# A hybrid retention, attention and expert layer on one core: instruction order from deadlines, with gathers held and small steps moved between engines

## The chip, the cores and the metric

The kernel runs on one core of one Trainium2 chip. The metric is device time in microseconds (us), the median over runs. The core has five engines, each with a queue of its own that it works through in order: TensorE (PE; its weight loads are PEld) for matmuls, VectorE (DVE), ScalarE (ACT), GpSimd (POOL) and SyncE (SP), which here only issues DMAs. GpSimd also issues the indirect DMAs that fetch rows by index.

## The reference

One layer over 1024 latent tokens and 256 context tokens of width 1024, in float32. A modulated RMS norm feeds one projection, whose columns go to four heads of bidirectional retention and four heads of differential attention; both outputs are joined, projected and added with a gate. Then each token goes through a product-key expert layer with 8 retrieval heads, 16 experts each out of 128 x 128, and a gated residual.

```python
rq, rk, rv, rg, dq, dk, dv = split(modulate(x, norm1_g, ...) @ w_in)
ret = rms_norm(bidirectional_retention(...)) * silu(rg)
dif = (softmax(q1 k1) - lam * softmax(q2 k2)) v          # per head, then rms_norm
x = x + mod[2] * (concat(ret, dif) @ w_out)
h2 = modulate(x, norm2_g, ...)
def peer_ffn(hb):                                         # 128 tokens at a time
    q = (hb @ w_query).reshape(t, 8, 2, 128)
    s = einsum('thpc,hpnc->thpn', q, sub_keys)
    v1, i1 = top_k(s[:, :, 0], 16); v2, i2 = top_k(s[:, :, 1], 16)
    cand = v1[..., :, None] + v2[..., None, :]            # 256 sums, ids i1 * 128 + i2
    best, pos = top_k(cand, 16)
    experts, gate = cand_idx[pos], softmax(best)
    act = gelu(einsum('thkd,td->thk', expert_u[experts], hb))
    return einsum('thk,thkd->td', gate * act, expert_v[experts])
x = x + mod[5] * peer_ffn(h2)
```

## The kernel before

Tokens are worked on in blocks of 128: 8 latent blocks, 2 of context. The code does not call the engines itself: a recorder, `Plan`, takes every instruction with an estimated cost, its dependencies and a priority. `schedule()` then plays the engines through a model (costs, DMA time, buffers that come free), lets each idle engine take its ready instruction of the lowest priority value, and so writes down the order in which each engine's queue is filled. That one pass is the order that runs. The priority of an instruction is the matmul time recorded before it, so the order in which the parts are recorded, woven into one another by the spans QSPAN, ASPAN, GSPAN, HSPAN and so on, sets the order of the work. All instructions pass through one helper, which is why every row of the profile has line L497; rows are told apart by the names of their tiles.

The parts, in the order of time:

- Projections (`project_half`, `late_queries`) in three float32r products of high and low parts each; `qk` normalizes and rotates queries and keys; `f_rg` makes the SiLU of the retention gate by Exp on ScalarE and an add, a reciprocal and a product on VectorE (tile u), and stores it. `retention` follows.
- Per group of blocks (GROUPS = [0], [4,5], [6,7], [3], [1,2]): `mix` (attention, output projection, second norm) and `route` (query projection, then `top16` per head with VectorE's top-8 instructions, then `select`). `select` forms 50 candidate sums per head, takes the best 16 and finds their ids: VectorE compares a row of 0 to 49 with each found position (16 x 50 elements), GpSimd multiplies by the ids, VectorE sums; 8 times a block, in tile sel.
- Blocks 3 to 7 (DENSE) go through all 128 x 128 experts by matmul. For that `gates` builds, from the ids, a matrix of gate values: for four tokens at a time a compare of the low id (o2) and of the high id times the gate weight (o1), four matmuls, four ScalarE copies into staging tiles; after 32 tokens four stores to Wd in DRAM. o2 is made on ScalarE (Abs, Relu) for every other four tokens (O2A), else by one wide VectorE compare; o1 by four VectorE compare-and-scale instructions. Tiles o, t, and pt for the ids.
- Blocks 0, 1 and 2 gather their experts' rows: `halves` issues 768 indirect DMAs of 128 rows (512 KB) on GpSimd into tile gat (4 buffers; tile h lends some). For an expert's u row VectorE multiplies with the tokens and sums (gat<-gat,h2t), for its v row it adds a scaled row to acc (acc<-gat,act,acc). These have priorities of their own, by a pace (POFF, PACES).
- `dense_phase`: 128 steps in groups of 4. `dense_act` loads one 128-expert part of u, splits it into high (ScalarE) and low parts (VectorE, tile h, 1024 wide), multiplies, applies Gelu, multiplies by the gate rows, and splits the result into high (ScalarE) and low (CL = 'P': GpSimd; tiles rv, 384 wide, and t, 256 wide). `dense_val` does the same with v (tile h, 512 wide; VL = 'PDD': every third low part on GpSimd, the others on VectorE) and adds the products to b and t.

In the planner's cost model VectorE instructions with two inputs in SBUF and GpSimd's arithmetic exclude each other.

## Time and profile before

| what | before |
|---|---|
| median of 3 runs | 3646.94 us (3646.93 to 3651.82) |
| profiled execution, its own time | 3638.93 us |
| its span | 3637.1 us |
| TensorE busy | 3254.3 us (89%) |
| VectorE busy | 2945.7 us (81%) |
| GpSimd busy | 1750.9 us (48%) |
| ScalarE busy | 1258.8 us (35%) |
| mean granted TensorE clock | 0.935 of full |
| DMA | 809.72 MB, 223 GB/s |

An engine's busy share is an average over stages that have different limits, so it has to be read by stage. In a row of an instruction form the columns are the names of output and inputs, the shapes, the count, the busy time and the mean duration of one in ns, and then the idle time just before such instructions with what ended it. Idle time counts only on the engine that sets the pace.

### The profile page before, as it was taken

How to read it: one execution, taken by the hardware profiler on the slowest of the kernel's cores; microseconds unless marked ns; L12 is line 12 of the kernel's file. 1: busy time of each engine (PE TensorE's matmuls, PEld its weight loads, DVE VectorE, ACT ScalarE, POOL GpSimd, SP SyncE). 2: the span in 40 equal slices, each digit the busy share in tenths (PEclk: the TensorE clock that was granted, in tenths of full speed). 3: DMA queues.
4: the chain of work that ended last, by engine and by line, in shares of the span. 5: the costliest groups of instructions: out<-in, count | busy, mean ns of one | idle time of the engine just before them, and what ended most of it. 6: DMA issues, size and time to landing. Idle time of an engine off the chain costs nothing. (4 is left out here: it accounts for less than half of the span.)

```text
span 3637.1 us, 52106 instructions
## 1 busy us (share of the span) xinstructions
PE 3254.3 (89%) x18240; PEld 2793.0 (77%) x18240; DVE 2945.7 (81%) x5999; ACT 1258.8 (35%) x3210; POOL 1750.9 (48%) x1457
## 2 busy tenths in 40 slices
PE   7989987888778658777889999999999999999998
PEld 4987566566667646566878898888988889898897
DVE  4456547879999899989798988889898979888954
ACT  4342333324226546566432222222222222222221
POOL 0101122555462242332067775767667657686731
PEclk9999988889988869788999999999999999999999
DMA  5223544777555735547547888888888888888943
GB/s 179 81 83 98 167 165 149 239 246 263 174 182 201 255 124 195 198 159 265 165 135 257 295 286 284 271 306 293 295 303 275 306 270 291 303 290 300 301 145 110
DMA packets 314536, 809.72 MB, mean 223 GB/s; under 512 B 29313, under 2 KB 125593, under 8 KB 314274
## 3 DMA queue, kind: packets, MB, share of 16 engines
q1 hardware_dynamic: 203682, 403.70, 33.3%
q0 software_dynamic: 110592, 402.70, 32.2%
q8 instruction: 144, 2.36, 0.3%
q14 instruction: 118, 0.97, 0.1%
HBM read 745.46 MB, written 60.83 MB: 222 GB/s over the span
## 5 line engine op out<-in xcount | busy, mean ns | idle before, releaser
L497 PE MATMUL mm<-k,h 128*128 128x384 f32 (+1 forms) x4096 | 888.7, 308 | 3.7 <-DVE h L497 3.7
L497 PEld LDWEIGHTS mm<-k,h 128*128 128x128 f32 x4096 | 688.2, 188 | 5.9 <-DVE h L497 4.4
L497 ACT CAST h<-wst 128x512 fp32r<-128x512 f32 (+1 forms) x384 | 292.1, 763 | 1085.0 <-PE mm L497 963.2
L497 POOL DMA_INDIRECT gat<-peer_v,egb x363 | 471.5, 1299 | 347.7 <-DVE acc L497 187.1
L497 PE MATMUL mm<-v,h 128*128 128x384 f32 (+1 forms) x2048 | 633.0, 309 | 0.0
L497 POOL DMA_INDIRECT gat<-peer_u,egb x345 | 448.2, 1299 | 369.6 <-DVE gat L497 232.5
L497 PE MATMUL mm<-h,rv 128*128 128x512 f32 x2304 | 584.2, 397 | 13.7 <-POOL rv L497 9.2
L497 DVE SCALAR_TENSOR_TENSOR acc<-gat,act,acc 128x1024 f32<-128x1024 f32 x360 | 522.6, 1452 | 48.0 <-DMA gat<-peer_v,egb 42.9
L497 PEld LDWEIGHTS mm<-h,rv 128*128 128x128 f32 x2304 | 431.0, 189 | 121.5 <-POOL rv L497 14.9
L497 DVE SCALAR_TENSOR_TENSOR gat<-gat,h2t 128x1024 f32<-128x1024 f32 x345 | 481.0, 1397 | 51.9 <-DMA gat<-peer_u,egb 51.6
L497 PE MATMUL mm<-h,t 128*128 128x512 f32 (+1 forms) x1600 | 418.0, 394 | 14.0 <-DVE b L497 13.3
L497 DVE TENSOR_TENSOR h<-wst,h 128x512 fp32r<-128x512 f32 (+1 forms) x298 | 336.2, 1134 | 88.9 <-ACT h L497 61.6
L497 PEld LDWEIGHTS mm<-v,h 128*128 128x128 f32 x2048 | 385.0, 188 | 1.3
L497 PEld LDWEIGHTS mm<-h,t 128*128 128x128 f32 x1600 | 299.2, 189 | 88.3 <-DVE b L497 16.5
L497 POOL TENSOR_TENSOR m<-m,mhalf 128x4 f32<-128x4 f32 (+1 forms) x78 | 76.4, 980 | 439.9 <-DVE m L497 435.6
L497 POOL TENSOR_TENSOR rv<-aT,rv 128x384 fp32r<-128x384 f32 x128 | 154.5, 1207 | 242.5 <-ACT rv L497 234.9
L497 PE MATMUL mm<-b,wst 128*128 128x256 f32 (+1 forms) x1280 | 250.9, 354 | 9.1 <-ACT rv L497 9.1
L497 PEld LDWEIGHTS mm<-b,wst 128*128 128x128 f32 x1280 | 214.0, 201 | 40.9 <-ACT rv L497 9.6
L497 POOL TENSOR_TENSOR sel<-sel 128x800 f32<-128x800 f32 (+6 forms) x120 | 136.8, 1156 | 214.7 <-DVE sel L497 200.5
L497 ACT COPY rv<-mm 128x128 f32<-128x128 f32 (+2 forms) x664 | 178.3, 412 | 113.3 <-PE mm L497 97.4
L497 PE MATMUL mm<-t,h 128*128 128x256 f32 x992 | 187.5, 288 | 7.9 <-ACT aT L497 3.3
L497 PE MATMUL mm<-k,t 64*128 64x512 f32 (+1 forms) x384 | 174.2, 620 | 22.8 <-ACT h L497 13.2
(235 smaller groups left out, 5454.6 us busy)
## 6 DMA issues: line engine op xcount, KB each, us to landing
wst<-peer_u_cols SPq DMA_DIRECT2D x128, 512.0 KB
wst<-peer_v_halves SPq DMA_DIRECT2D x128, 512.0 KB
wst<-w_query_chunks SPq DMA_DIRECT2D x80, 512.0 KB
Wd<-rv SPq DMA_DIRECT2D x80, 512.0 KB
h<-Wd SPq DMA_DIRECT2D x64, 512.0 KB
wst<-w_mod_chunks SPq DMA_DIRECT2D x48, 512.0 KB
wst<-w_out_chunks SPq DMA_DIRECT2D x40, 512.0 KB
wst<-w_in_chunks SPq DMA_DIRECT2D x32, 512.0 KB
```

Of the source, the lines that this page charges most:

```text
L497: getattr(handles[n.eng], meth)(*[res(v) for v in a], **k)
```

## The change

Eight edits. (1) The priorities come from a plan: `plan()` runs `schedule()` up to four times (PASSES); after each, `ahead()` goes backwards through that pass and gives every instruction the mean of its start and its latest start, over dependencies and over buffers handed on; the pass with the shortest planned span is kept. The weaving spans are set anew. (2) While the planner's clock is between 1000 and 1600 us (HOLD), GpSimd may take no gather. (3) In `gates` both compares are one wide VectorE instruction each, and the gate weight is multiplied in by four ScalarE copies with a scale. (4) The staging tiles of `gates` alternate between rv and gat. (5) `f_rg` uses ScalarE's SiLU. (6) In `select` the ids are found by a keyed minimum: each candidate's id gets 32768 times its place added, 32768 times the found place is subtracted, and the minimum of the absolute value over 50 is the id; GpSimd's product falls away. (7) All low parts of the dense phase are on VectorE (VL, CL = 'D'). (8) `qk` and `head_norm` put their squares into SBUF rather than PSUM. The gathers have an order of buffers of their own (key rows); EXTRA is empty. No matmul is added or removed.

```diff
+STEP = 32768
+PASSES = 4
+HOLD = [1000, 1600]
+EXTRA = [[], [], []]
...
-QSPAN = [[-0.2, 0.475], [0.1, 1], [-0.2, 1.309], [-0.6, 1.05], [0, 0.85]]
+QSPAN = [[-0.2, 0.475], [0.1, 1], [-0.05, 1.309], [-0.35, 1.05], [0.15, 0.9]]
...
-VL, CL, EC, EM, XE = 'PDD', 'P', 'PD', 'P', 'PPPPPPPP'
+VL, CL, EC, XE = 'D', 'D', 'PD', 'PPPPPPPP'
...
-O2A = [0, 2, 4, 6]
...
@@ in schedule()
-                pick = None
+                pick, held = None, []
                 while avail[e]:
                     item = heapq.heappop(avail[e])
                     m = nodes[item[1]]
+                    if e == "POOL" and m.xfer and HOLD[0] <= t < HOLD[1]:
+                        held.append(item)
+                        continue
...
                 if pick is None:
+                    if held:
+                        heapq.heappush(events, HOLD[1])
...
+                n.done = done
...
+    def ahead(self, out):
+        left, freed, used, succ = {}, {}, {}, {}
+        for bs in self.order.values():
+            for b in bs:
+                left[id(b)] = len(b.nodes)
+        taken = set()
+        for n in out:
+            pred = set(n.deps)
+            for b in n.bases:
+                if b.dram or id(b) in taken:
+                    continue
+                taken.add(id(b))
+                used[b.tag] = used.get(b.tag, 0) + 1
+                if used[b.tag] > self.bufs.get(b.tag, 1):
+                    pred |= freed[b.tag].pop(0)
+            for b in n.bases:
+                if not b.dram:
+                    left[id(b)] -= 1
+                    if left[id(b)] == 0:
+                        freed.setdefault(b.tag, []).append(b.nodes)
+            for q in pred:
+                succ.setdefault(q, []).append(n)
+        latest = {}
+        for n in sorted(out, key=lambda n: (n.start, n.seq), reverse=True):
+            took = n.done - n.start
+            latest[n.seq] = min([self.span - took] + [latest[x.seq] - took - SEM for x in succ.get(n.seq, ())
+                                                      if x.seq in latest])
+        for n in out:
+            n.prio = (n.start + latest[n.seq]) / 2
+    def plan(self):
+        best = None
+        for i in range(PASSES):
+            if i:
+                self.ahead(out)
+                for bs in self.order.values():
+                    for b in bs:
+                        if b.lenders:
+                            b.tag = b.key
+            try:
+                out = self.schedule()
+            except RuntimeError:
+                break
+            tags = {id(b): b.tag for bs in self.order.values() for b in bs}
+            if best is None or self.span < best[0]:
+                best = (self.span, out, tags)
+        self.span, out, tags = best
+        for bs in self.order.values():
+            for b in bs:
+                b.tag = tags[id(b)]
+        return out
...
-        sch = self.schedule()
+        sch = self.plan()
...
+        steps = sb([128, NCAND], "steps")
+        nc.vector.tensor_scalar(steps, iota[:, :NCAND], float(STEP), None, op0=OP.mult)
...
         def f_rg(kb, pm, c):
-            t = sb([128, 256], "u4")
-            nc.scalar.activation(t, pm, AF.Exp, scale=-1.0)
-            nc.vector.tensor_scalar(t, t, 1.0, None, op0=OP.add)
-            nc.vector.reciprocal(t, t)
-            nc.vector.tensor_tensor(out=t, in0=t, in1=pm, op=OP.mult)
+            t = sb([128, 256], "fin")
+            nc.scalar.activation(t, pm, AF.Silu)
             nc.sync.dma_start(rgd[kb - NCB][:, c * 256:(c + 1) * 256], t)
...
         def qk(kb, pm, which, h0):
             m4 = sb([128, 2, 4], "m4")
-            sq = ps([128, 256])
-            nc.scalar.activation(sq, pm, AF.Square, scale=SC)
+            xn = sb([128, 256], "u1")
+            nc.scalar.activation(xn, pm, AF.Square, scale=SC)
...
         def head_norm(dst, src, gain):
-            sq = ps([128, 512])
-            nc.scalar.activation(sq, src, AF.Square)
+            nc.scalar.activation(dst, src, AF.Square)
...
-            nc.vector.tensor_copy(posf, pos)
+            nc.vector.tensor_scalar(posf, pos, float(STEP), None, op0=OP.mult)
+            nc.vector.tensor_tensor(out=cid, in0=cid, in1=steps[:, None, :].to_broadcast([128, PH, NCAND]), op=OP.add)
             for h in range(PH):
                 oh = sb([128, TK, NCAND], "sel")
-                nc.vector.tensor_tensor(out=oh, in0=iota50[:, None, :].to_broadcast([128, TK, NCAND]),
-                                        in1=posf[:, h, :, None].to_broadcast([128, TK, NCAND]), op=OP.is_equal)
-                eng(EM, h).tensor_tensor(out=oh, in0=oh, in1=cid[:, h:h + 1, :].to_broadcast([128, TK, NCAND]), op=OP.mult)
-                nc.vector.tensor_reduce(out=ef[:, h, :], in_=oh, axis=AX.X, op=OP.add)
+                nc.vector.tensor_tensor(out=oh, in0=cid[:, h:h + 1, :].to_broadcast([128, TK, NCAND]),
+                                        in1=posf[:, h, :, None].to_broadcast([128, TK, NCAND]), op=OP.subtract)
+                nc.vector.tensor_reduce(out=ef[:, h, :], in_=oh, axis=AX.X, op=OP.min, apply_absolute_value=True)
...
-        def gather(rows, table):
+        def gather(b, rows, table):
             t = sb([128, D], "gat")
-            t.base.lenders = LENDERS
+            t.base.key, t.base.lenders = "rows", LENDERS + EXTRA[b]
             nc.gpsimd.indirect_dma_start(out=t, out_offset=None, in_=table, in_offset=(rows,))
             return t
...
-                stage = [sb([128, 32, TG], "rv") for _ in range(4)]
+                stage = [sb([128, 32, TG], "gat" if g % 2 else "rv") for _ in range(4)]
                 for q in range(TG // 4):
                     t0 = g * TG + q * 4
                     o2 = sb([128, 4, 128], "t3" if q % 2 else "t6")
                     pm = ps([128, 4, 128])
-                    if q in O2A:
-                        for j in range(4):
-                            nc.scalar.activation(o2[:, j, :], iota, AF.Abs, scale=-1.0,
-                                                 bias=pt[:, 1, t0 + j:t0 + j + 1])
-                        nc.scalar.activation(o2, o2, AF.Relu, scale=-1.0, bias=1.0)
-                    else:
-                        nc.vector.tensor_tensor(out=o2, in0=iota[:, None, :].to_broadcast([128, 4, 128]),
-                                                in1=pt[:, 1, t0:t0 + 4, None].to_broadcast([128, 4, 128]),
+                    o1 = sb([128, 4, 128], "t4" if q % 2 else "o")
+                    for o, x in ((o1, 0), (o2, 1)):
+                        nc.vector.tensor_tensor(out=o, in0=iota[:, None, :].to_broadcast([128, 4, 128]),
+                                                in1=pt[:, x, t0:t0 + 4, None].to_broadcast([128, 4, 128]),
                                                 op=OP.is_equal)
-                    o1 = sb([128, 4, 128], "t4" if q % 2 else "o")
                     for j in range(4):
-                        t = t0 + j
-                        nc.vector.tensor_scalar(o1[:, j, :], iota, pt[:, 0, t:t + 1], pt[:, 2, t:t + 1],
-                                                op0=OP.is_equal, op1=OP.mult)
+                        nc.scalar.activation(o1[:, j, :], o1[:, j, :], AF.Copy, scale=pt[:, 2, t0 + j:t0 + j + 1])
                     with nc.unit():
                         for j in range(4):
                             nc.tensor.matmul(pm[:, j, :], o2[:, j, :], o1[:, j, :], start=True, stop=True)
```

## Rows read from the trace of the kernel before

**Rows 1.** Stretches: busy PE, PEld, DVE, ACT, POOL (instructions); clock, DMA share, GB/s
```profile
0.00:600.00 600.00, 534.53 (x3629) 437.78 (x3629) 310.34 (x837) 210.55 (x526) 73.82 (x101) 0.94 0.42 136
600.00:1800.00 1200.00, 922.24 (x4665) 743.29 (x4666) 1075.68 (x3090) 570.80 (x1770) 469.48 (x398) 0.84 0.59 204
1800.00:3637.00 1837.00, 1797.49 (x9948) 1611.92 (x9946) 1559.67 (x2074) 477.45 (x914) 1207.62 (x959) 0.99 0.78 263
```
**Rows 2.** TensorE's waits, 600 to 1800: us in total, times, longest
```profile
PE mm L497 <- DVE t L497: 62.5, 27, 8.2
PE mm L497 <- ACT rv L497: 31.7, 13, 6.2
...
PE mm L497 <- DVE s L497: 0.2, 1, 0.2
```
**Rows 3.** Instructions in order of time, 2600 to 2621: start, duration, idle before
```profile
2601.57 1.27 DVE L497 SCALAR_TENSOR_TENSOR acc<-gat,act,acc 128x1024 f32<-128x1024 f32 x1
2604.29 1.21 DVE L497 SCALAR_TENSOR_TENSOR gat<-gat,h2t 128x1024 f32<-128x1024 f32 x1
...
2618.95 0.42 DVE L497 TENSOR_TENSOR u<-u,h 128x256 f32<-128x256 f32 x1
...
2619.77 1.61 POOL L497 TENSOR_TENSOR rv<-aT,rv 128x384 fp32r<-128x384 f32 x1 [0.83 <-ACT rv L497]
2620.43 2.04 DVE L497 SCALAR_TENSOR_TENSOR gat<-gat,h2t 128x1024 f32<-128x1024 f32 x1
```
**Rows 4.** Instructions that read the gathers' ids (egb), 1000 to 1600: DVE, POOL, clock, DMA
```profile
1000.00:1600.00 600.00, 0.00 (x0) 98.44 (x82) 0.80 0.54 185
```
**Rows 5.** VectorE's instructions by form, 600 to 1800: busy, mean ns, idle before
```profile
L497 DVE TENSOR_SCALAR t<-iota,pt 128x128 f32<-128x128 f32 x320 | 111.6, 404 | 0.0
...
L497 DVE TENSOR_TENSOR t<-iota,pt 128x512 f32<-128x512 f32 x80 | 58.5, 731 | 11.0 <-PE mm L497 10.7 <-issue 0.2
```
**Rows 6.** The same of ScalarE, 600 to 1800
```profile
L497 ACT COPY rv<-mm 128x128 f32<-128x128 f32 x640 | 169.5, 414 | 71.7 <-PE mm L497 55.9 <-DMA Wd<-rv 15.3
L497 ACT ACTIVATE t<-iota,pt 128x128 f32<-128x128 f32 x320 | 109.4, 395 | 84.8 <-PE mm L497 84.4 <-ACT u L497 0.4
...
L497 ACT ACTIVATE t<-t 128x512 f32<-128x512 f32 x80 | 50.5, 631 | 2.0
```
**Rows 7.** What SP's queue waited for, 600 to 1800
```profile
SPq L497 <- ACT rv L497: 232.8, 27, 33.1
```
**Rows 8.** VectorE's reciprocals in the gate of retention, 600 to 1800
```profile
L497 DVE RECIPROCAL u<-u x10: 1741/1753/1754, 707.7 to 1028.7; 128x256 f32<-128x256 f32 x10
```
**Rows 9.** ScalarE's table loads in the whole span
```profile
L497 ACT ACT_TABLE_LOAD x12 | 15.4, 1283 | 11.0 <-DVE sel L497 5.8 <-DMA cc<-c_ctx 4.3 <-PEq L1511 0.7
```
**Rows 10.** GpSimd's products of the ids, 600 to 1800
```profile
L497 POOL TENSOR_TENSOR sel<-sel 128x800 f32<-128x800 f32 x48 | 89.8, 1871 | 183.9 <-DVE sel L497 171.1 <-issue 6.1 <-DVE m L497 3.3
```
**Rows 11.** GpSimd by form, 1900 to 3500: its subtractions
```profile
L497 POOL TENSOR_TENSOR rv<-aT,rv 128x384 fp32r<-128x384 f32 x112 | 136.1, 1216 | 25.9 <-ACT rv L497 18.3 <-issue 5.1
...
L497 POOL TENSOR_TENSOR h<-wst,h 128x512 fp32r<-128x512 f32 x75 | 106.8, 1424 | 16.2 <-ACT h L497 15.1
```
**Rows 12.** VectorE by form, 1900 to 3500
```profile
L497 DVE SCALAR_TENSOR_TENSOR acc<-gat,act,acc 128x1024 f32<-128x1024 f32 x314 | 460.3, 1466 | 47.5 <-DMA gat<-peer_v,egb 42.9 <-issue 3.0 <-DVE h L497 0.3
L497 DVE SCALAR_TENSOR_TENSOR gat<-gat,h2t 128x1024 f32<-128x1024 f32 x253 | 357.1, 1412 | 39.4 <-DMA gat<-peer_u,egb 39.1
L497 DVE TENSOR_TENSOR h<-wst,h 128x512 fp32r<-128x512 f32 x152 | 151.6, 1006 | 20.9 <-ACT h L497 18.6 <-DMA out<-fin 2.3
...
L497 DVE TENSOR_TENSOR b<-b,mm 128x512 f32<-128x512 f32 x227 | 143.8, 680 | 18.0 <-PE mm L497 17.7
```
**Rows 13.** As rows 4, in stretches of the dense stage
```profile
1800.00:1900.00 100.00, 3.40 (x3) 5.63 (x5) 1.00 0.33 101
1900.00:3400.00 1500.00, 2.58 (x5) 710.33 (x541) 1.00 0.85 289
...
3500.00:3600.00 100.00, 0.00 (x0) 0.00 (x0) 1.00 0.28 85
```

More of the change, by code (lines that the diff above doesn't have):

```diff
@@ L33 @@
 LATE = [2, 4, 7]
-QSPAN = [[-0.2, 0.475], [0.1, 1], [-0.2, 1.309], [-0.6, 1.05], [0, 0.85]]
-ASPAN = [[0.05, 1.424], [0, 1.05], [-0.1, 1], [0, 1.104]]
-GSPAN = [[0.3, 1], [-0.15, 0.754], [0.15, 1.248], [0.05, 1.2], [0, 0.02]]
+QSPAN = [[-0.2, 0.475], [0.1, 1], [-0.05, 1.309], [-0.35, 1.05], [0.15, 0.9]]
+ASPAN = [[0.05, 1.424], [0, 1.05], [0.15, 1], [0, 1.104]]
+GSPAN = [[0.3, 1], [-0.15, 0.754], [0.15, 1.248], [-0.1, 1.2], [0, 0.02]]
 DSPAN = [0.02, 0.0, 0.05]
-LSPAN = [[0.479, 1.05], [0.265, 0.918], [0.136, 1.3], [0.05, 1]]
+LSPAN = [[0.479, 1.05], [0.565, 1.218], [0.436, 1.3], [0.05, 0.85]]
 G2SPAN = [0.182, 0.991]
-VL, CL, EC, EM, XE = 'PDD', 'P', 'PD', 'P', 'PPPPPPPP'
+VL, CL, EC, XE = 'D', 'D', 'PD', 'PPPPPPPP'
 POFF, PACES = 40, [[0, 3.6], [200, 3.0], [300, 1.17], [700, 1.18], [1100, 1.9]]
@@ L48 @@
 NS4 = 25
-W0 = [0.552, 1.035]
-HSPAN = [[0.05, 1.15], [0.05, 0.796], [0.2, 1.388]]
+W0 = [0.552, 1.085]
+HSPAN = [[-0.25, 0.85], [0.05, 0.796], [0.2, 1.538]]
 XT = ['gat'] * 5
@@ L127 @@
     __slots__ = ("eng", "calls", "cost", "deps", "prio", "seq", "bases", "xfer", "table", "ports",
-                 "succ", "wait", "ready", "start")
+                 "succ", "wait", "ready", "start", "done")
 class Proxy:
@@ L429, in schedule @@
                     heapq.heappush(parked[tag], (at,) + item)
+                for item in held:
+                    heapq.heappush(avail[e], item)
                 if pick is None:
+                    if held:
+                        heapq.heappush(events, HOLD[1])
                     continue
@@ L543, in layer @@
                        allow_small_or_imprecise_dtypes=True)
-        iota50 = iota[:, :NCAND]
+        steps = sb([128, NCAND], "steps")
+        nc.vector.tensor_scalar(steps, iota[:, :NCAND], float(STEP), None, op0=OP.mult)
         mhalf = sb([128, 16], "mhalf")
@@ L819, in qk @@
             m4 = sb([128, 2, 4], "m4")
-            sq = ps([128, 256])
-            nc.scalar.activation(sq, pm, AF.Square, scale=SC)
-            nc.vector.tensor_reduce(out=m4[:, 0, :], in_=sq.rearrange("p (g d) -> p g d", g=4), axis=AX.X, op=OP.add)
+            xn = sb([128, 256], "u1")
+            nc.scalar.activation(xn, pm, AF.Square, scale=SC)
+            nc.vector.tensor_reduce(out=m4[:, 0, :], in_=xn.rearrange("p (g d) -> p g d", g=4), axis=AX.X, op=OP.add)
             rstd(m4[:, 1, :], m4[:, 0, :])
-            xn = sb([128, 256], "u1")
             nc.vector.tensor_tensor(out=xn.rearrange("p (g d) -> p g d", g=4),
@@ L894, in head_norm @@
         def head_norm(dst, src, gain):
-            sq = ps([128, 512])
             m4 = sb([128, 2, H], "m4")
-            nc.scalar.activation(sq, src, AF.Square)
-            nc.vector.tensor_reduce(out=m4[:, 0, :], in_=sq.rearrange("p (h e) -> p h e", h=H), axis=AX.X, op=OP.add)
+            nc.scalar.activation(dst, src, AF.Square)
+            nc.vector.tensor_reduce(out=m4[:, 0, :], in_=dst.rearrange("p (h e) -> p h e", h=H), axis=AX.X, op=OP.add)
             nc.vector.tensor_scalar(m4[:, 0, :], m4[:, 0, :], 1.0 / 128, None, op0=OP.mult)
@@ L1260, in u_step @@
                 h2, act, _ = st[b]
-                t = gather(eidx[b][:, r:r + 1], u2)
+                t = gather(b, eidx[b][:, r:r + 1], u2)
                 nc.vector.scalar_tensor_tensor(t, t, 1.0, h2, op0=OP.mult, op1=OP.mult, accum_out=act[:, r:r + 1])
@@ L1269, in v_step @@
                 _, act, acc = st[b]
-                t = gather(eidx[b][:, r:r + 1], v2)
+                t = gather(b, eidx[b][:, r:r + 1], v2)
                 cf = act[:, r:r + 1]
```

## The prediction

> **What bounds the kernel now.** Three views, in this order. First the busy times by stage [rows 1]: I cut the span where the shares change. Stage A, 0 to 600 us (projections), has TensorE busy 89% at a mean clock of 0.94, VectorE about half busy. Stage C, from 1800 us on (the dense experts), has TensorE busy 98% at 0.99: nothing but less matmul work would shorten it, and the change removes no matmul. Stage B between them (retention's end, attention, routing, gate rows, and the first gathers) has TensorE busy only 922 of 1200 us at a mean clock of 0.84, and VectorE busy 1076 of 1200, or 90%. So the time to be had lies in B, and there VectorE is the fullest engine.
>
> Second, whom TensorE waits for in B [rows 2]: 278 us idle in all. Adding up the listed waits by engine, ten groups on VectorE (from t, 62.5, to s, 0.2) make 124 us, six on ScalarE (the largest, rv, the gate rows' staging, 31.7) 91 us, three on GpSimd 53 us; 10 us are left for all else, loads among them. The clock stands on two levels, 1.2 and 2.4 GHz; a mean of 0.84 means half speed for about a third of B. 922.24 x 0.84 = 775 us would be its work at full speed, so 147 us of its busy time is paid to the low clock, which sets in where TensorE has stood idle. Per us of idle that is 147 / 278 = 0.53 us more.
>
> Third, the instructions on VectorE and GpSimd, with one thing to see: two forms that overlap. The same product of a gathered row took 1.21 us alone and 2.04 us where a GpSimd subtraction (1.61 us, itself stretched) ran beside it [rows 3]. GpSimd's arithmetic costs VectorE about 0.83 / 1.61 = 0.5 us for each us. Gather issues beside an instruction of the same kind did not show this.
>
> **The change part by part, stage B.** *Gathers held.* In B's middle, 1000 to 1600 us, 82 gathers are issued [rows 4]. The change forbids them in such a stretch of the planner's time, which I read as the same stretch of the trace; by how much the two clocks differ the trace can't show (bounds: none to all 82 leave B). Each brings VectorE at least 1.24 us (1.27 for v, 1.21 for u [rows 3]): 82 x 1.24 = 102 us leave B and come back in C.
>
> *Gate rows.* 640 small compare-and-scale instructions in two rows alike, each 320 in 111.6 us, and 80 wide compares in 58.5 us [rows 5] make 282 us. They become 320 wide compares at 0.731: 234 us. Gain 48 us. ScalarE loses 320 Abs and 80 Relu, 109.4 + 50.5 = 160 us, and gains 640 scaled copies; nearest row the Abs with its operand pointer, 0.342 us: 219 us [rows 6]. So ScalarE gets 59 us more, at 571 of 1200 busy [rows 1], but a compare now passes VectorE, then ScalarE, then TensorE. I let 15 us of the 59 appear as waits (bounds 0 and 59).
>
> *Second staging set.* ScalarE stood 15.3 us for the Wd stores to free the staging rows [rows 6]; half of it back, 8 us (bounds 0 and 15). Each group also issues four stores on SP, and SP stood 233 us at such stores for ScalarE [rows 7], holding the loads queued behind them. They move with the order of the gates. Loads stand among the 10 us of TensorE's other waits, so I cost this at nothing, and at up to 33 us, the longest such stand, if the loads' lead is gone.
>
> *SiLU on ScalarE.* Ten reciprocals of 1.75 us in B go [rows 8], 17.5 us; the add and the product beside them I leave uncounted. The Exp becomes a SiLU of the same size. New table loads: one load took 1283 ns, 12 in the whole run [rows 9]. Sixteen SiLUs can cost no load or up to 32, 0 to 41 us; I take none as visible, since ScalarE is half idle.
>
> *Ids.* 48 products of 1.87 us leave GpSimd in B [rows 10], 90 us, and with them 0.5 us each of VectorE's time: 45 us. VectorE's own two steps keep their size; two short steps per block are added, a few us in all. VectorE now runs its pair without waiting for GpSimd. Here a rule of the Trainium skill gives another size. Its page "SBUF — State Buffer", section "Who interferes with whom", says that VectorE with two SBUF inputs and a GpSimd instruction that reads SBUF exclude each other for the whole instruction. By it the relief would be the whole 90 us, not 45, and the forecast 27 us lower (3479 instead of 3506), still inside the forecast's own range. The one pair of rows (0.83 us for 1.61) lies between no cost and a whole block, and I stay with the rows.
>
> Together VectorE loses 102 + 48 + 17 + 45 = 212 of 1076 us, a fifth. I let two thirds of its waits go, 83 of 124 us: a fifth less load on an engine at 90% triples its free share, but some waits are chains that no freer engine shortens. GpSimd's 53 us have two parts: its own arithmetic on TensorE's path stays, the gathers and products queued ahead of it go; I take half, 26. ScalarE's 91 grow by 15 - 8 = 7. Idle removed: 83 + 26 - 7 = 102; with the clock, 102 x 1.53 = 156 us.
>
> *Order by deadlines; squares in SBUF instead of PSUM.* The trace of before shows neither. Nearest: A, where 65 us of idle stay with VectorE half free. I take 0 for A and for the order itself; bounds: B as well fed as A (first rival) on one side, the fourth rival on the other.
>
> **Stage C.** The low parts leave GpSimd: in 1600 us, which hold 112 of the 128 steps, 112 of width 384 (rv), as many of width 256 (t), and 75 of v [rows 11]. On VectorE they cost 75 x 0.68 (a 512-wide row) = 51, and 112 x (0.55 + 0.42) = 109; 0.42 is the row of 256, and 0.55 for 384 an estimate between 256 and 512 [rows 3, 12]. Scaled by 128/112, 183 us. Against that stands the overlap that goes: v products 314 x (1.466 - 1.27), u products 253 x (1.412 - 1.21), v low parts 152 x (1.006 - 0.68) [rows 3, 12]: 62 + 51 + 50, scaled 185 us. So the move costs VectorE nothing on balance. The held gathers add 82 x 1.28 = 105: 1560 becomes about 1663 of 1837, 91% instead of 85%. TensorE hides it as long as VectorE keeps ahead; with the cover gone it is the third rival. Their issue: 541 gathers in 1900 to 3400, 36 per 100 us; 82 more are 228 us. Room is there at both ends, 5 gathers in 1800 to 1900 and none in 3500 to 3600 [rows 13], some 95 + 105 us. What is over I set at +15 us (bounds 0 and the second rival).
>
> **Sum.** The profiled run took 3638.93 us, 1.8 more than its span; 3638.93 - 156 + 15 = 3498. The median of the runs is 8 us above that run, so **3506 us**, 3.9% faster; its own range 3430 to 3580. What is late next: in B the chain compare, scale, matmul, and softmax on ScalarE; in C the last gathers.
>
> **Rivals.**
> 1. *B as well fed as A*: the order by deadlines closes most gaps. For it: VectorE at 864 us has room. Against: B's chains are longer. A's efficiency is 534.53 x 0.94 / 600 = 0.84; B then takes 775 / 0.84 = 923, -277 us: 3385 us. Chance 0.14.
> 2. *Gain partly given back by the gathers*: no room at C's start is used, so 228 - 105 = 123 us of them run behind the last matmuls. For it: DMA busy 0.85 in C already [rows 13]. 3506 + 108 = 3614 us. Chance 0.12.
> 3. *Slower: low parts queue behind gathered rows in C.* VectorE takes its instructions in order; a product waiting for its row now holds the value rows' low parts, 256 of them, and TensorE needs each. If each comes one product (1.28 us) late beyond the staged lead: +328 us, 3834. It decides from (3647 - 3506) / 256 = 0.55 us each, where the forecast's gain is gone. Against: two thirds already stood there and TensorE was 98% busy. Chance 0.14.
> 4. *The order is not renewed*: no later pass plans shorter, the first is kept, and only the edits remain; half of B's gain, -78: 3584 us. Chance 0.11.
> 5. *Everything cancels*: within 0.2%. Chance 0.05.
>
> **How the numbers follow.** The forecast has the remaining 0.44. Faster by over 0.2%: 0.44 + 0.14 + 0.12 + 0.11 = 0.81; within 0.2% (about what a measurement of this kernel can tell from no change) 0.05; slower 0.14. For 8 in 10 the range leaves out the third rival and the lower half of the first: 3380 to 3650.
>
> **What would show it.** Right: in B less than 900 us of VectorE, TensorE's waits for VectorE under 50 us, granted clock near 0.9, no gathers in a stretch of some 600 us; wide compares near 0.73 or below; in C no GpSimd subtraction, v products near 1.28 us, TensorE still 98%. Wrong: TensorE in C under 95%, with waits for VectorE's h, rv or t (third rival); gathers after the last matmul (second); B as long as before with VectorE at 70% (the chain, not the load, was the bound); more than 25 table loads.

## The result, and the profile after

The changed kernel takes 3478.97 us (median of four runs, 3468.12 to 3483.45) against 3647.15 us for the kernel before: ratio 0.9532, 95% interval 0.9506 to 0.9557, so 4.7% faster. The forecast was 3506 us, the range 3380 to 3650. The kernels of the study ran beside fresh runs of the kernel before, between 3638 and 3640 us; ratios are compared, and 0.01 is 36 us. A ratio's interval reaches some 4 to 14 us to either side, so a difference of less than about 10 us says nothing.

Two landmarks cut the kernels better than a fixed time. The first is TensorE's first matmul of the dense activations (mm<-k,h), which ends stage B; its last one nearly ends the kernel. Their rows give count, duration min/median/max in ns, and first and last start. Before, then after, and the kernel before's and after's stores of the first residual (x1d), whose first marks the end of stage A:

```profile
L497 PE MATMUL mm<-k,h x4096: 277/335/525, 1789.3 to 3598.6; 128*128 128x384 f32 x98, 128*128 128x256 f32 x98
L497 SPq DMA_DIRECT2D x1d<-b x8: 326/326/327, 527.0 to 1637.9; - x8
```

```profile
L563 PE MATMUL mm<-k,h x4096: 277/335/689, 1579.6 to 3426.5; 128*128 128x384 f32 x98, 128*128 128x256 f32 x98
L563 SPq DMA_DIRECT2D x1d<-b x8: 319/323/423, 489.9 to 1451.9; - x8
```

The dense stage starts 210 us earlier, 37 of which were already won when the first residual was stored, and it takes 1847 us instead of 1809. So A gave 37, B 173, and the dense stage took 37 back. The landmark is the first dense matmul, not the end of the waiting: in the 150 us behind it TensorE stands idle for 31 us, against 14 before, most of it for low parts that VectorE makes late. Its longest wait there, from 1579 to 1730 us:

```profile
PE mm L563 <- DVE rv L563: 18.2, 1, 18.2
```

So some 17 of the 37 us are this start.

The stages of the changed kernel, cut at 600 and at the dense stage's start (columns as in [rows 1]), and of the kernel before with the same cut:

```profile
0.00:600.00 600.00, 531.68 (x3702) 438.94 (x3703) 323.12 (x930) 231.31 (x567) 84.36 (x120) 0.96 0.43 142
600.00:1580.00 980.00, 853.51 (x4554) 690.10 (x4553) 829.76 (x2429) 601.20 (x1983) 271.31 (x248) 0.91 0.58 199
1580.00:3427.00 1847.00, 1787.15 (x9870) 1594.76 (x9869) 1541.95 (x2488) 478.16 (x909) 833.26 (x684) 0.99 0.83 283
```

```profile
600.00:1789.00 1189.00, 913.36 (x4617) 734.81 (x4618) 1070.18 (x3077) 569.01 (x1767) 469.48 (x398) 0.84 0.59 203
```

In B VectorE's work fell from 1070 to 830 us, 240 us; the prediction had taken out 212. In A it rose by 13. TensorE's clock rose from 0.84 to 0.91, and its idle time fell from 276 to 126 us. Whom TensorE still waits for there (answers [rows 2]):

```profile
PE mm L563 <- DVE t L563: 19.8, 8, 4.5
PE mm L563 <- ACT o L563: 17.3, 11, 3.6
...
PE mm L563 <- POOL b L563: 5.8, 3, 2.9
...
PE mm L563 <- ACT rv L563: 2.2, 4, 0.6
```

Added up by engine as before: VectorE 58 us (before 124), ScalarE 47 (91), GpSimd 11 (53). The wait for the staging tiles (ACT rv, 31.7 us in [rows 2]) is nearly gone, also counted with the copies that now go to gat (3.1 us).

The gathers' issues (answers [rows 4, 13]; VectorE, GpSimd, clock, DMA) stand still for 596 us, then run to the end:

```profile
1020.00:1616.00 596.00, 0.52 (x2) 0.00 (x0) 0.92 0.48 162
1616.00:1700.00 84.00, 0.52 (x2) 29.11 (x25) 0.86 0.65 219
1700.00:3300.00 1600.00, 1.16 (x5) 737.92 (x584) 1.00 0.85 291
3300.00:3430.00 130.00, 0.00 (x0) 56.57 (x47) 0.99 0.84 282
```

VectorE in the dense stage, 1900 to 3300 us (answers [rows 12]), and the wide compares and the table loads in the whole span (answer [rows 5, 6, 9]):

```profile
L563 DVE SCALAR_TENSOR_TENSOR acc<-gat,act,acc 128x1024 f32<-128x1024 f32 x259 | 331.7, 1281 | 33.8 <-DMA gat<-peer_v,egb 32.8
L563 DVE SCALAR_TENSOR_TENSOR gat<-gat,h2t 128x1024 f32<-128x1024 f32 x249 | 303.9, 1221 | 35.1 <-DMA gat<-peer_u,egb 34.9
...
L563 DVE TENSOR_TENSOR h<-wst,h 128x512 fp32r<-128x512 f32 x193 | 129.6, 687 | 15.8 <-ACT h L563 15.4
...
L563 DVE TENSOR_TENSOR rv<-aT,rv 128x384 fp32r<-128x384 f32 x97 | 53.9, 556 | 6.7 <-ACT rv L563 5.8 <-issue 0.9
...
L563 DVE TENSOR_TENSOR t<-u,t 128x256 fp32r<-128x256 f32 x96 | 40.3, 420 | 0.3 <-ACT t L563 0.3
```

```profile
L563 DVE TENSOR_TENSOR t<-iota,pt 128x512 f32<-128x512 f32 x240 | 177.2, 772 | 13.3 <-PE mm L563 13.2
...
L563 ACT ACTIVATE o<-o,pt 128x128 f32<-128x128 f32 x320 | 108.4, 406 | 12.9 <-DVE o L563 12.8
...
L563 ACT ACT_TABLE_LOAD x28 | 35.9, 1283 | 13.7 <-DVE m L563 8.6 <-DVE sel L563 3.1 <-issue 1.0
```

Some of the marks that the prediction named for being right were not met: TensorE's waits for VectorE in B are 58 us (under 50 named), a wide compare takes 0.772 us (0.73 or below), and TensorE is busy 97% of the dense stage (1787 of 1847 us; 98%). The 28 table loads are one of its marks of being wrong (more than 25).

With no subtraction left on GpSimd in the dense stage, a v product takes 1.281 us (1.466 before) and the 512-wide subtraction 0.687, beside some 500 gather issues. The Trainium skill's page "SBUF — State Buffer", section "Who interferes with whom", sets GpSimd instructions that read SBUF against VectorE's with two SBUF inputs, not those that only write. Which of the two a gather's issue is, no run here shows. The trace shows that it costs VectorE nothing: from 1900 to 3300 us a v product takes 1.28 us in the median beside a gather's issue and 1.28 without, a u product 1.22 and 1.22.

### The profile page after: what moved, and what is told of

Read it like the earlier page. It is cut to its first block, busy times and chain, and to the rows that moved or that the text cites. A ratio compares the mean times of both kernels' runs of the same rounds, so it can differ in the third digit from the quotient of the medians.

```text
span 3466.0 us, 51310 instructions
## 1 busy us (share of the span) xinstructions
PE 3200.0 (92%) x18240; PEld 2745.9 (79%) x18240; DVE 2724.9 (79%) x5902; ACT 1315.0 (38%) x3466; POOL 1188.9 (34%) x1051
## 5 line engine op out<-in xcount | busy, mean ns | idle before, releaser
L563 PE MATMUL mm<-k,h 128*128 128x384 f32 (+1 forms) x4096 | 916.7, 310 | 20.7 <-DVE h L563 13.3
L563 POOL DMA_INDIRECT gat<-peer_v,egb x377 | 498.1, 1321 | 598.7 <-DVE acc L563 425.2
L563 PE MATMUL mm<-h,rv 128*128 128x512 f32 x2304 | 594.8, 397 | 23.8 <-DVE rv L563 22.5
L563 POOL DMA_INDIRECT gat<-peer_u,egb x360 | 421.5, 1171 | 547.8 <-DVE gat L563 287.5
L563 DVE SCALAR_TENSOR_TENSOR acc<-gat,act,acc 128x1024 f32<-128x1024 f32 x375 | 480.4, 1281 | 46.2 <-DMA gat<-peer_v,egb 44.7
L563 DVE SCALAR_TENSOR_TENSOR gat<-gat,h2t 128x1024 f32<-128x1024 f32 x360 | 450.8, 1255 | 52.6 <-DMA gat<-peer_u,egb 52.1
L563 PE MATMUL mm<-b,wst 128*128 128x256 f32 (+1 forms) x1280 | 242.1, 346 | 3.3 <-ACT b L563 1.5
L563 DVE TENSOR_TENSOR b<-b,mm 128x512 f32<-128x512 f32 x248 | 166.3, 684 | 77.6 <-PE mm L563 77.0
L563 ACT CAST rv<-aT 128x384 fp32r<-128x384 f32 x128 | 65.8, 514 | 329.1 <-DVE aT L563 315.9
L563 DVE TENSOR_TENSOR t<-iota,pt 128x512 f32<-128x512 f32 x240 | 177.2, 772 | 13.3 <-PE mm L563 13.2
```

The costliest lines, as they stand in the source:

```text
L563: getattr(handles[n.eng], meth)(*[res(v) for v in a], **k)
```

## The experiments

The theory of the prediction is called the load theory: B got shorter because VectorE lost work there, the order by itself brings nothing, and in the dense stage moving the low parts is an even trade. The main rival is the order theory.

**The moved steps alone, then with the hold.** Both runs keep the first plan's order; the second gets the hold.

```diff
-PASSES = 4
-HOLD = [1000, 1600]
+PASSES = 1
+HOLD = [0, 0]
```

> The changed kernel with PASSES = 1 and no hold: the moved steps, staging sets and spans alone, in the first plan's order. The first plan with the hold took 3547 us. If the hold itself is worth what the prediction's shares say (75 us in B against 37 later): 3585 us. If it is worth the 80 us that its removal cost with the renewed order: 3625 us, and then the moved steps are worth only some 20. If its removal harmed the renewal alone: 3540 to 3560 us.

Measured: 3610.83 us, ratio 0.9923 (0.9903 to 0.9942). The changed kernel with PASSES = 1 and the hold kept:

> The changed kernel with PASSES = 1: all edits stay, but the first pass with its hand-woven priorities is the order that runs; nothing is renewed by deadlines. Load theory (the prediction's: stage B shortened because VectorE lost some 212 us of work there, the order itself brings nothing): at most 3500 us, about 3479 plus the 20 to 30 us by which the first projections ended earlier. Order theory (the renewed order brings most of the 168 us, the load moved only gave it room): 3580 us or more.

Measured: 3546.60 us, ratio 0.9738 (0.9721 to 0.9754). The dense activations and the residual's stores, of the moved steps alone, then with the hold:

```profile
L563 PE MATMUL mm<-k,h x4096: 277/309/529, 1757.2 to 3569.1; 128*128 128x384 f32 x98, 128*128 128x256 f32 x98
L563 SPq DMA_DIRECT2D x1d<-b x8: 320/326/424, 522.5 to 1628.4; - x8
```

```profile
L563 PE MATMUL mm<-k,h x4096: 277/308/525, 1650.2 to 3508.7; 128*128 128x384 f32 x98, 128*128 128x256 f32 x98
L563 SPq DMA_DIRECT2D x1d<-b x8: 320/327/424, 522.7 to 1521.1; - x8
```

The moved steps bring the dense stage's start from 1789 to 1757, the hold to 1650, the renewed order to 1580. In the ratios that is 0.8%, another 1.9%, another 2.1% (75 us). So the order has a large share, against the load theory, and stage A's gain is the order's: the first residual is stored at 522 us in both runs and at 490 with the renewed order. With the hold the dense stage is 47 us longer (1859 against 1812), but not in its course: TensorE has one long wait for a low part right behind the landmark (from 1650 to 1800 us), where the moved steps alone have 46.8 us:

```profile
PE mm L563 <- DVE h L563: 93.2, 2, 92.6
```

VectorE is 94% busy then, with gathered products and the last of `select`. So the landmark comes early in this run, and the ratio has the hold's size.

The hold also frees more than VectorE. The second staging set lies in gat, whose four buffers the gathers use. In B of the moved steps alone (600 to 1757 us) TensorE's longest waits are for copies into it:

```profile
PE mm L563 <- ACT gat L563: 91.0, 8, 31.8
```

With the hold they are 1.0 us. TensorE's idle time in B falls by 86 us between the two runs (251 to 166), and this one wait by 90. So without the hold edit 4 exchanged a wait of 32 us (ACT rv, [rows 2]) for one of 91, which is likely much of why the moved steps alone bring so little. Both runs also have the new weaving spans and the gathers' own order of buffers; neither was added or undone alone, and their share is open.

**The order alone.** The kernel before with `ahead`, `plan` and PASSES = 4, nothing else.

> The kernel before with the passes and deadlines added and nothing else: same steps, same engines, same spans, no hold. Load theory: within 15 us of 3647, since VectorE is as full in stage B as before. Order theory: 3560 us or less. Between 3580 and 3630 both have a share.

Measured: 3640.15 us, ratio 1.0 (0.9990 to 1.0010). This says less than it seems: the planner's passes gave spans of 3488, 3520, 3537 and 3542, so the first was kept, and the kernel before ran again. On the old steps the renewal finds nothing that its own model would take. In the changed kernel the spans are 3457, 3400, 3388 and 3378, and the fourth is kept; the 79 that it plans to win over the first came out as 75 us.

**The hold and the order on the old steps.** The kernel before with the hold added as well; its second pass is kept.

> The kernel before with the hold and the renewed order, and every step as before. Load theory: the gathers' 102 of the 212 us leave stage B and 37 us come back in the dense stage: 3647 - 75 + 37, about 3605 us. Order theory (given the hold, the renewal brings what it brought in the changed kernel, some 70 us more): 3550 us or less. If the old steps leave the order no room: 3630 us or more.

Measured: 3764.19 us, ratio 1.0340 (1.0320 to 1.0360): 124 us slower than before, which neither theory had. The dense activations, and whom TensorE waited for from 1700 to 3700 us:

```profile
L562 PE MATMUL mm<-k,h x4096: 277/334/690, 1705.4 to 3724.9; 128*128 128x384 f32 x98, 128*128 128x256 f32 x98
```

```profile
PE mm L562 <- POOL rv L562: 70.7, 27, 5.4
PE mm L562 <- DVE h L562: 48.7, 9, 13.3
PE mm L562 <- POOL t L562: 31.8, 14, 5.0
```

The dense stage did start 84 us earlier, as the load theory wants, though 28 of these were won in A; it got longer by 210, with TensorE waiting 103 us for GpSimd's low parts and 49 for VectorE's.

**The hold taken out of the changed kernel.** HOLD = [0, 0], four passes.

> The changed kernel without the stretch in which gathers are held. Load theory: some 80 gathers come back into stage B, 100 us of VectorE there; by the prediction's shares B gets 102/212 of 156 = 75 us longer and the dense stage regains its 37 us: about 3517 us, and TensorE's waits for VectorE in B rise by some 40 us. Order theory: the deadlines put the gathers where they do no harm, 3470 to 3490 us.

Measured: 3558.34 us, ratio 0.9771 (0.9754 to 0.9787), 87 us slower than the changed kernel. In B and in the dense activations:

```profile
600.00:1674.00 1074.00, 875.05 (x4622) 710.30 (x4622) 942.32 (x2578) 619.74 (x2007) 375.66 (x338) 0.88 0.65 225
```

```profile
L563 PE MATMUL mm<-k,h x4096: 277/334/687, 1674.5 to 3526.0; 128*128 128x384 f32 x98, 128*128 128x256 f32 x98
```

VectorE has 112 us more in B (predicted 102), and B is 94 us longer (predicted 75). But VectorE's load is not the only thing that changed. TensorE is idle for 72 us more in B (199 against 126), and 41 of them are again the copies into gat, 3.1 us in the changed kernel; behind them ScalarE waits 33 us until VectorE is done with gathered rows in these buffers:

```profile
PE mm L563 <- ACT gat L563: 44.1, 8, 14.2
```

So the hold wins by VectorE's load and by the tiles that it leaves to the staging; the two were not separated. The dense stage is not shorter (1852 us), but it starts with 65 us of idle TensorE in its first 150, against 31, so its length does not tell what the held gathers cost. One reservation: without the hold the renewal came to a stop after its second pass, so this run has a little less order too. The first residual is stored at 504 us instead of 490, so some 15 of the 87 us lie in A.

**One staging set.** All stage tiles from rv.

```diff
-stage = [sb([128, 32, TG], "gat" if g % 2 else "rv") for _ in range(4)]
+stage = [sb([128, 32, TG], "rv") for _ in range(4)]
```

> The changed kernel with the gate rows staged in the rv tiles alone, as before; order planned anew. The prediction's 8 us: 3480 to 3495. Rival, the stores set the pace of the gate rows once the rest is faster: each group of 32 tokens waits until four stores have read the tiles, and stage B gets longer by 60 us or more, 3540 us or more, with ScalarE waiting for Wd's stores.

Measured: 3588.58 us, ratio 0.9861 (0.9844 to 0.9877), 120 us slower: the rival, and more.

```profile
600.00:1665.00 1065.00, 884.96 (x4623) 718.44 (x4622) 837.58 (x2439) 622.35 (x2007) 263.20 (x250) 0.89 0.52 183
```

```profile
PE mm L563 <- ACT rv L563: 20.2, 8, 6.3
```

VectorE has the same work in B as in the changed kernel (838 against 830 us), and B is 85 us longer: here the load theory fails. But ScalarE does not wait for the stores either, as the rival expected; the order was planned around the shortage. TensorE's wait for the staging copies is back at 20 us (the second row, 900 to 1700 us). Some 14 of the 85 us lie in A, as its second pass is the one kept (first residual at 504 us); which of many places in B carries the other 50 is open. The dense stage is longer too, and has one wait of 75 us for VectorE's h at its start. The plan shows most of the price beforehand: its span is some 112 us longer than the changed kernel's.

**The ids as before.** `select` with compare, GpSimd's product and sum.

> The changed kernel with the ids found as before: compare on VectorE, product on GpSimd, sum on VectorE; order planned anew. Load theory: 90 us of GpSimd's products return to stage B and with them 45 us of VectorE's time, 45/212 of 156 us: some 33 us slower, 3500 to 3525. If the overlap is no matter there: 3470 to 3490.

Measured: 3535.87 us, ratio 0.9712 (0.9693 to 0.9731), 66 us slower, twice the load theory's 33.

```profile
600.00:1625.00 1025.00, 858.39 (x4578) 706.12 (x4577) 865.84 (x2412) 605.89 (x1988) 336.05 (x278) 0.90 0.52 181
```

VectorE gets 36 us in B (predicted 45). B gets 45 us longer, but 15 of them lie in A: here too the second pass is the one kept, and the first residual is stored at 505 us. From there to the dense stage it is 30 us more, close to the 33. The dense stage takes the rest, with 68 us of idle TensorE in its first 150. Size and sign of the load are right; whether the chain of eight times VectorE, GpSimd, VectorE costs more than its load, these runs do not show.

**The compares as before.** o1 by four small compare-and-scale instructions, o2 by ScalarE or VectorE in turn.

> The changed kernel with the gate rows' compares as before: o1 by four small compare-and-scale instructions on VectorE, o2 by ScalarE or VectorE in turn; the two staging sets stay; order planned anew. Load theory: 48 us of VectorE's work return to stage B and 59 us leave ScalarE: 48/212 of 156 us, some 35 us slower less the few that ScalarE gains, 3495 to 3520. If not VectorE's sum in B but the waits at single places decide (as the staging set's 115 us for a predicted 8 suggest): 3470 to 3490.

Measured: 3484.85 us, ratio 0.9570 (0.9544 to 0.9596). The interval overlaps that of the changed kernel: no difference that these runs can tell.

```profile
600.00:1576.00 976.00, 840.63 (x4568) 683.58 (x4567) 835.36 (x2831) 555.19 (x1744) 260.43 (x253) 0.92 0.57 198
```

```profile
L564 DVE TENSOR_SCALAR t<-iota,pt 128x128 f32<-128x128 f32 x320 | 100.6, 367 | 0.0
```

VectorE has 835 us in B, not 48 more. The small instructions took 101 + 99 us instead of 112 + 109, perhaps because GpSimd is busy there for 260 us instead of 469 (not tested), and the new compares cost 0.772 and 0.760 instead of 0.731. The edit saves 19 us of VectorE and gives ScalarE 46.

**The low parts on GpSimd, order kept.** Instruction by instruction the changed kernel's order; after planning, the low parts (`moved`: all of tiles rv and t, every third of v) are handed to GpSimd's queue.

```diff
         sch = self.plan()
...
+        for n in self.nodes:
+            if n.seq in moved:
+                n.eng = "POOL"
```

> The changed kernel with its order kept instruction by instruction, but the low parts of the dense stage handed to GpSimd as before (every third of the value rows, all of the activations). Even-trade theory (the prediction's: 183 us of VectorE's work against 185 us of overlap): VectorE's busy time in the dense stage within 30 us of the changed kernel's, time 3465 to 3495 us. Rival, VectorE as pace: its queue holds the low parts back in the changed kernel, so the dense stage gets shorter by up to the 37 us that it lost, 3440 to 3460. Rival, cost of overlap: products stretched from 1.27 to about 1.45 us push VectorE over TensorE, 3510 us or more.

Measured: 3643.94 us, ratio 1.0019 (1.0004 to 1.0035). The whole gain is gone, in the dense stage alone (B's landmark stays at 1582). TensorE's and GpSimd's longest waits from 1900 to 3300 us, and the v products:

```profile
PE mm L578 <- POOL rv L578: 45.7, 19, 5.6
PE mm L578 <- POOL t L578: 38.1, 18, 5.0
```

```profile
POOL gat L578 <- DVE acc L578: 260.3, 99, 17.4
POOL gat L578 <- DVE gat L578: 167.6, 83, 7.3
```

```profile
L578 DVE SCALAR_TENSOR_TENSOR acc<-gat,act,acc 128x1024 f32<-128x1024 f32 x229 | 337.8, 1475 | 34.2 <-DMA gat<-peer_v,egb 33.0
```

The products are stretched to 1.475 us as expected, yet VectorE is only 80% busy (1115 of 1400 us), so it is not VectorE's total that costs. GpSimd is 63% busy and stands 428 us before gathers whose buffer VectorE has not yet freed. That is not what holds the low parts up: the kernel before stands 289 us at gathers in the same stretch, with low parts in the same queue, and TensorE waits 9 us for them. Behind TensorE's 84 us of waits for rv and t, the low parts started 173 us in all after their input was ready. Of these 94 went to issuing gathers, 52 to other subtractions and only 26 to a gather that waited for its buffer. One of them on GpSimd's queue; the last row's input was ready at 2344.0, and TensorE waited for it for 5.05 us:

```profile
2345.15 1.28 POOL L578 TENSOR_TENSOR h<-wst,h 128x512 fp32r<-128x512 f32 x1
2347.79 1.70 POOL L578 DMA_INDIRECT gat<-peer_v,egb  x1 [1.36 <-DVE acc L578]
2349.79 0.94 POOL L578 DMA_INDIRECT gat<-peer_u,egb  x1 [0.30 <-issue]
2350.75 1.14 POOL L578 TENSOR_TENSOR t<-u,t 128x256 fp32r<-128x256 f32 x1
```

So the low parts do stand in the queue, mostly behind work that is being done. They are also longer there (rv 1.18 us and t 1.12, on VectorE 0.56 and 0.42), and VectorE's own steps on TensorE's path are stretched (aT<-aT,t from 0.29 to 0.54 us). How the cost divides among these is not shown. The time is in the dense stage, as in the third case, but not in VectorE's pace; none of the cases had named the queue.

**The low parts on GpSimd, order made for it.**

```diff
-VL, CL, EC, XE = 'D', 'D', 'PD', 'PPPPPPPP'
+VL, CL, EC, XE = 'PDD', 'P', 'PD', 'PPPPPPPP'
```

> The changed kernel with the low parts of the dense stage on GpSimd as before, and the order planned anew for that, in four passes. With the changed kernel's order kept, the same move cost 174 us, with TensorE waiting for GpSimd's rv and t. Queue theory (there the low parts stood behind gathers that waited for a buffer; an order made for it puts them ahead): 3470 to 3500 us, TensorE 98% busy in the dense stage. Engine theory (two kinds of work in GpSimd's one queue cost this in any order): 3560 us or more.

Measured: 3621.20 us, ratio 0.9947 (0.9929 to 0.9965). Planning for it helps by little, while the planner's own span puts this kernel only some 26 us behind the changed one. The dense activations:

```profile
L563 PE MATMUL mm<-k,h x4096: 277/334/687, 1577.0 to 3556.9; 128*128 128x384 f32 x98, 128*128 128x256 f32 x98
```

Yet the kernel before has the low parts on GpSimd too, and a dense stage of 1809 us. What differs is TensorE's own sequence. Counted from the traces around 2550 us, matmuls of activations (A) and values (V) in turn:

```
before:         A 192, V 120, A 192, V 120
changed kernel: A 144, V 78, A 12, V 9, A 12, V 15, A 12, V 12, A 12, V 6, A 144
this run:       A 132, V 75, A 12, V 9, A 12, V 12, A 12, V 12, A 12, V 9, A 12, V 3, A 132
first plan:     A 192, V 120, A 192
```

The renewed order weaves the next group's activations into the values. The pace in 16 dense steps, from ScalarE's splits of u and v: 228 us before, 224 with the first plan, 230 in the changed kernel, 247 here.

**The dense sequence kept.** The renewed priorities with one rule more: each dense matmul has at least the priority value of the one recorded before it.

```diff
             n.prio = (n.start + latest[n.seq]) / 2
+        wide = [n for n in self.nodes if n.eng == "PE" and n.calls[0][0] == "matmul" and n.calls[0][1][1].dtype == F32R]
+        first = min(n.seq for n in wide if n.calls[0][1][2].base.tag in ("k", "v"))
+        least = 0.0
+        for n in sorted(wide, key=lambda n: n.seq):
+            if n.seq >= first:
+                least = n.prio = max(n.prio, least + 0.001)
```

> The changed kernel with one rule added to the renewed priorities: TensorE's matmuls of the dense stage keep the sequence in which they are recorded (192 for the activations, 120 for the values, in turn), where the changed kernel's order weaves them in pieces of 3 to 144. Sequence theory (the weaving takes the lead from the steps between, and so the dense stage's pace went to 230 us per 16 steps, against 224 with the first plan): pace 224, the stage about 45 us shorter, 3420 to 3445 us. Rival (the pace is lost to the gathers that the hold moved there and to VectorE's load): pace 229 to 230 still, 3465 to 3490 us.

Measured: 3435.86 us, ratio 0.9442 (0.9426 to 0.9457), 33 us faster than the changed kernel, 5.6% faster than the kernel before, and the fastest of the study. The same rule with the low parts on GpSimd:

> The same rule in the kernel whose low parts are on GpSimd with the order renewed (3621 us, pace 247 us per 16 steps). Sequence theory: GpSimd's low parts were late only because the woven order left them no lead; pace back to the 228 of the kernel before, 3480 to 3510 us. Engine theory (gathers and low parts in GpSimd's one queue cost this whatever TensorE's sequence): 3590 us or more. Between 3530 and 3570 both have a share.

Measured: 3529.50 us, ratio 0.9710 (0.9671 to 0.9749), 86 us faster than without the rule. The dense activations of the two, and TensorE's longest wait of the second from 1900 to 3300 us:

```profile
L569 PE MATMUL mm<-k,h x4096: 279/335/687, 1582.4 to 3396.7; 128*128 128x384 f32 x98, 128*128 128x256 f32 x98
```

```profile
L569 PE MATMUL mm<-k,h x4096: 279/311/426, 1570.9 to 3481.9; 128*128 128x384 f32 x98, 128*128 128x256 f32 x98
```

```profile
PE mm L569 <- POOL rv L569: 40.6, 19, 5.0
```

With the rule the dense stage takes 1814 us on VectorE's low parts, 33 less, and 1911 on GpSimd's, 69 less. The pace is 226 in the first, where the sequence theory had 224, and 238 in the second, where it had 228. Both causes are there: the weaving costs either kernel, and even in sequence low parts on GpSimd cost 97 us more than on VectorE. The kernel before has them on GpSimd in sequence at 1809 us. What makes the other 102 us, the renewed order of the gathers, the gathers that were held or something else, was not tested.

## Why the prediction was right

The sign, the range and the size held: 3506 forecast, 3479 measured. The stage was right: B gained 173 us where 156 were forecast. The dense stage did take something back (37, predicted 15), and rivals 2 and 4 did not come about: the last gather is issued at 3423 us, before the last dense matmul, and the fourth pass was kept. Rival 3, low parts that stand behind gathered rows in VectorE's queue, came about at the dense stage's start alone, where TensorE waits some 30 us for them; from 1900 to 3300 us it waits 10 us for VectorE's t, rv and h. The experiments show that the total was partly right by errors that offset each other:

- *The load of VectorE in B*: 212 us predicted, 240 measured. Hold 102, measured 112. Compares 48, measured 19: the term was mis-sized, because both old and new forms came out at other costs than in the rows (and the two rows of small compares, called alike, are 111.6 and 108.9 us, which makes 45).
- *The ids*: 45 predicted, 36 measured, near by luck: the 0.5 us per us that they rest on was read wrongly. Beside the product of 2.04 us stood not one subtraction but two, the one of [rows 3] and this one behind it:

```profile
2621.34 1.72 POOL L497 TENSOR_TENSOR t<-u,t 128x256 fp32r<-128x256 f32 x1
```

The product began 0.66 us behind the first subtraction and ended 1.09 us after that one's end (alone it takes 1.21); the second subtraction ended 0.59 us after the product (alone it takes 0.73). From 1900 to 3300 us of the kernel before, 43 u products began while a subtraction ran and took 1.97 us in the mean; 40 of them took the rest of the subtraction and 1.21 us, to within 0.15 us. The 58 that began first took 1.21 us. This agrees, pair by pair, with the Trainium skill's rule of a whole block (page "SBUF — State Buffer", section "Who interferes with whom"). The 90 us that the prediction drew from the rule do not follow: only the instruction that begins second waits, and GpSimd's busy time holds its own waits.

- *From load to time*: I let a fifth less work free 83 of 124 us of waits; 66 went. TensorE's waits for GpSimd fell by 42, where I took 26, and those for ScalarE by 44, where I let them grow by 7. So the 102 us of idle time that I removed were 150. In the kernel before and the runs with two staging sets, B is 1.11 to 1.23 times VectorE's work (before 1189/1070, moved steps alone 1157/983, no hold 1074/942, old ids 1025/866, changed 980/830, first plan with hold 1050/852). So the two go together, but that does not show load as the whole cause: with one staging set the ratio is 1.27 (1065/838), and without the hold 41 us of B's waits are the tiles of the staging.
- *The order at nothing*: wrong. It is worth 75 us, 33 of them in stage A, which I had set at 0. On the moved steps without the hold a renewed pass still brought 55 us (0.9923 to 0.9771); on the old steps the planner found nothing.
- *The second staging set at 8 us*: wrong by far; taking it away costs 120. The step that failed is the reading of ScalarE's 15.3 us of waits for stores as the whole price. It also left out that the gathers hold gat's buffers, so that TensorE waits 91 and 44 us for the second set in the two runs without the hold.
- *The low parts as an even trade*: right in VectorE's busy time (1543 us of the dense stage before, 1542 after; I had said 1663, and the overlap that went was worth more than the three forms that I had priced), wrong as a statement on time. Undone, it costs 151 us with the order made for it and 177 with the order kept. There TensorE waits for low parts that come late through GpSimd's queue, which I had not priced; what the queue, the longer low parts and VectorE's stretched steps each cost is open.
- *The dense stage's 37 us*: not the gathers' issue, as I had it. The woven sequence costs 33 us and the waits at the start some 17, so the rest of the stage got some 13 shorter. (The room for gathers at its start, 31 of the usual 36, was 86 us and not 95.)
- *Table loads*: 28, where I had named 25 as the mark of a miss. Sixteen more make 21 us of ScalarE; SiLU was not undone alone, nor were the squares in SBUF, so their shares stay open.

What each undone edit costs (hold 87, order 75, staging 120, ids 66, low parts 151) adds up to 499 us, three times the gain. They are not shares of one sum, since one edit is a condition for another, as the hold seems to be for the second staging set (two sets without the hold cost TensorE 91 and 44 us of waits). In the other direction, from the kernel before, the moved steps, the hold and the order added 28, 67 and 75 us. The planner's own spans had most of these prices: some 105 us for the hold, 79 for the order, 112 for the staging and 75 for the ids. They had only 26 for the low parts, and nothing for the weaving, whose rule won 33.

## What to carry to other kernels

A step that another engine waits for costs more than its own time on a queue that it shares: what is queued ahead of it counts too. Look at what stands between a step's input and its start before an engine's busy share decides where the step goes. Before a step gets tiles of another kind of work, look at who holds them, and when. An edit that shows no price alone can be what lets another one pay, so undo edits from the finished kernel as well as adding them to the old one. A planner's priorities from deadlines may take away lead that its model does not value; where an engine is the bound already, keep its sequence.

## What the runs showed of the hardware

A VectorE product of two SBUF inputs and a GpSimd subtraction did not slow each other in part: the one that began second waited for the first. In the kernel before a u product that began during a subtraction took 1.97 us in the mean, one that began ahead of it 1.21 us, the time alone. The issue of a gather of 128 rows took GpSimd at least 0.94 us and 1.17 to 1.34 in the mean, and beside it the products took no longer. The cost of the same VectorE instruction was not the same in two kernels: a product of a gathered v row took 1.28 us without and 1.48 us with subtractions on GpSimd, the small compare-and-scale 0.31 us of busy time each in one kernel and 0.35 in another.
